# Deferring the merge of the two branches behind the sending of the softmax sums in a hybrid decoder layer

## The chip, the core and the metric

The kernel runs on one core of one Trainium2 chip. The metric is device time in microseconds (us) of one execution. TensorE is called PE, VectorE DVE, ScalarE ACT, GpSimd POOL and SyncE SP; SP computes nothing, it issues DMA transfers in its order. A line number (L1363) is one of the kernel before.

## What is computed

The layer is a half-step SwiGLU FFN, then two token mixers on one normalised input (a gated DeltaNet and a sparse attention), merged by sigmoid gates, then a second half-step FFN and a final RMSNorm; 1024 tokens, width 1024, 8 heads of 128. What the change touches is the end of the attention branch and the merge:

```
p = softmax(logits)            # per head and query, over the kept keys
o_sa = (p @ latent) @ w_uv     # per head
merged = sigmoid(gate_a) * o_dn + sigmoid(gate_b) * o_sa
x = x + merged @ w_o
```

## The kernel before, in words

Everything lies transposed in SBUF: channels on the 128 partitions, tokens along the free axis. The gated DeltaNet's output (`odd`), its gate product (`zgd`) and the attention gate (`gbd`) were written to DRAM in an earlier stage, as 8 heads x 128 x 1024.

The attention stage (`mixer`, its last block) runs `attn_head` for the 8 heads. One head handles 1024 queries in four units of 256 queries, in the order g = 0, 1, 3, 2; unit g has 2g+2 blocks of keys, so g = 3 is the longest and g = 0 the shortest. In a unit, for two blocks of 128 queries: PE makes the logits (`pl`), DVE adds bias and mask and takes the maximum (L1322), ACT makes the exponentials and their sums (`a_sum`, L1327). Then, for pairs of key blocks, PE transposes the probabilities (`pp`, L1335), ACT rounds them to the high part `ph` (L1338), DVE makes the rest `plo` (L1339), and PE multiplies by the values into `pao` (L139 to L141). ACT copies the unit's result to `osa` (L1344). The bias tile `nb` (L1309) is made by POOL. The probabilities are not divided by their sum; that is done in `merge`.

After units g = 1 and g = 2, when four of the eight query blocks have their sums, `merge` handles half a head, 512 queries. DVE makes `a_r` = 0.5 / sum as a 128 x 4 column tile (L1354, L1355), with queries on the partitions. The result `osa` has channels on the partitions, so the row of 512 values must stand on every partition: SP writes `a_r` to DRAM (`a_rd`, L1357; 512 packets of 4 bytes) and reads it back to all 128 partitions (`a_rb`, L1361, 256 KB). SP also loads `od`, `zg` and `gb` (256 KB each, L1361). POOL multiplies `od` by `zg` (L1362), DVE multiplies `osa` by `a_rb` (L1363) and by `gb` + 1 (L1364), POOL adds both into `merged` (tile `mr`, L1365). The landing tiles `od`, `zg`, `gb` and `a_rb` have one buffer each.

Around it: `attn_values` makes the values for two heads at once (weights `w_uv`, loaded to `w_raw` with two buffers, rounded by ACT at L111 and split by POOL at L112 to `wa`); `attn_qk` makes the next head's queries and keys (weights `w_uq`, `w_uk`), traced after unit g = 1 with a priority that moves it ahead. After the last head `merged` is split into high and low parts (`mh`, `ml`), and `out_proj` multiplies by `w_o` (`pwo`, L1377 adds it to `x`).

The order of instructions on each engine and on SP's queue is not the order of the source: the framework traces all of it and then places the instructions by priority (source order, if nothing else is said) and by the readiness that its own timeline forecasts. On the chip each engine, and SP, then runs its list in that order and waits where an operand is late. `issue_after(ins)` adds an edge for order alone: what is traced inside, on the engine of `ins`, is placed behind `ins`.

Of the kernel before, what the change touches and what calls it, by code (L numbers as in the profile page):

```python
# [10 lines left out]
F32 = mybir.dt.float32  # L11
# [4 lines left out]
ALU = mybir.AluOpType  # L16
# [4 lines left out]
P = 128  # L21
# [6 lines left out]
H = 8  # L28
# [42 lines left out]
class Layer:  # L71
# [1223 lines left out]
    def attn_head(self, hd, p, ps, qk, values, merged, ahead):  # L1295
        nc = self.nc
        near = self.near_tile(p, hd)
        (qh, ql), (kh, kl) = qk
        vh, vl = values
        hv = slice((hd % 2) * P, (hd % 2) * P + P)  # L1300
        sums = self.stat.tile([P, NT], F32, name="a_sum")
        osa = p.tile([P, S], F32, name="osa", tag="osa", bufs=2)
        for g in (0, 1, 3, 2):
            probs = []
            for b in (2 * g, 2 * g + 1):
                W = (b + 1) * P
                n_near = min(W, 256)
                nb = p.tile([P, 256], F32, name="nb", tag="nb", bufs=4)
                nc.gpsimd.tensor_add(nb[:, 256 - n_near:], near[:, 256 - n_near:], self.mask[b][:, W - n_near:W])  # L1309
                s = self.slot(("w_hi", "w_lo")[b % 2])  # L1310
                mx = self.stat.tile([P, 4], F32, name="a_mx", tag="a_mx", bufs=3)
                m = 0
                for n0 in range(0, W, 512):
                    n1 = min(W, n0 + 512)
                    pl = ps.tile([P, 512], F32, name="pl", tag="lg")
                    self.mm3(pl[:, 0:n1 - n0], qh[b // 4][:, ts(b % 4, P)], ql[b // 4][:, ts(b % 4, P)], kh[n0 // 512][:, 0:n1 - n0],
                             kl[n0 // 512][:, 0:n1 - n0], True, True)
                    for a0, a1 in ((n0, min(n1, W - n_near)), (max(n0, W - n_near), n1)):
                        if a1 <= a0:
                            continue  # L1320
                        add = nb[:, a0 - W + 256:a1 - W + 256] if a0 >= W - n_near else self.mask[b][:, a0:a1]
                        nc.vector.tensor_tensor_reduce(s[:, a0:a1], pl[:, a0 - n0:a1 - n0], add, 1.0,  # L1322
                                                       mx[:, m - 1:m] if m else -3.0e38, ALU.add, ALU.max, accum_out=mx[:, m:m + 1])
                        m += 1
                nm = self.stat.tile([P, 1], F32, name="a_nm", tag="a_nm", bufs=3)
                nc.vector.tensor_scalar_mul(nm, mx[:, m - 1:m], -1.0)
                nc.scalar.activation(s[:, 0:W], s[:, 0:W], AF.Exp, bias=nm, accum_out=sums[:, b:b + 1])  # L1327
                probs.append(s)
            po = ps.tile([P, 512], F32, name="pao", tag="ao")
            for j in range(0, 2 * g + 2, 2):  # L1330
                pt = ps.tile([P, 512], F32, name="pp", tag="pt")
                blocks = [(j, 0), (j, 1), (j + 1, 0), (j + 1, 1)] if j < 2 * g else [(j, 0), (j, 1), (j + 1, 1)]
                n = len(blocks) * P
                for i, (jj, b) in enumerate(blocks):
                    nc.tensor.transpose(pt[:, ts(i, P)], probs[b][:, ts(jj, P)], self.ident)  # L1335
                ph = p.tile([P, 512], F32R, name="ph", tag="ph", bufs=3)
                pl_ = p.tile([P, 512], F32R, name="plo", tag="plo", bufs=3)
                nc.scalar.copy(ph[:, 0:n], pt[:, 0:n])  # L1338
                nc.vector.tensor_sub(pl_[:, 0:n], pt[:, 0:n], ph[:, 0:n])  # L1339
                for i in range(2):  # L1340
                    a, b = (0, 256) if i == 0 else (256, n)
                    out = po[:, 0:256] if b - a == 256 else po[:, 128:256]
                    self.mm3(out, vh[:, j + i, hv], vl[:, j + i, hv], ph[:, a:b], pl_[:, a:b], j + i == 0, j + i == 2 * g + 1)
            nc.scalar.copy(osa[:, ts(g, 256)], po[:, 0:256])  # L1344
            if g == 1:
                ahead()
            if g in (1, 2):
                self.merge(hd, g // 2, sums, osa, p, ps, merged)

    def merge(self, hd, h, sums, osa, p, ps, merged):  # L1350

        nc = self.nc
        r = self.stat.tile([P, 4], F32, name="a_r")
        nc.vector.reciprocal(r, sums[:, ts(h, 4)])  # L1354
        nc.vector.tensor_scalar_mul(r, r, 0.5)  # L1355
        rd = self.dram.tile([512], F32, name="a_rd", tag="a_rd", bufs=2)
        nc.sync.dma_start(rd.rearrange("(t i) -> i t", i=P), r)  # L1357
        od, zg, gb, rb = (p.tile([P, 512], F32, name=n, tag=n, bufs=1) for n in ("od", "zg", "gb", "a_rb"))
        v = ts(h, 512)
        for x, src in ((od, self.odd[hd][:, v]), (zg, self.zgd[hd][:, v]), (gb, self.gbd[hd][:, v]), (rb, rd.partition_broadcast(P))):  # L1360
            nc.sync.dma_start(x, src)  # L1361
        nc.gpsimd.tensor_mul(od, od, zg)  # L1362
        nc.vector.tensor_mul(osa[:, v], osa[:, v], rb)  # L1363
        nc.vector.scalar_tensor_tensor(osa[:, v], gb, 1.0, osa[:, v], ALU.add, ALU.mult)  # L1364
        nc.gpsimd.tensor_add(merged[:, v], od, osa[:, v])  # L1365


    def out_proj(self, m, ps, after_tile, after_half):
# [53 lines left out]
    def run(self):  # L1422
        nc, tc, I = self.nc, self.tc, self.I
# [4 lines left out]
        self.zgd = dt([H, P, S], F32, name="zgd")  # L1428
        self.gbd = dt([H, P, S], F32, name="gbd")
        self.odd = dt([H, P, S], F32, name="odd")  # L1430
        self.parts, self.B = {}, {}
        hs = ExitStack()
        self.open_parts(hs, "hT", 0, NK, "right")
        with ExitStack() as c:
            ps = Banks(self.psum, s=(0, 1, 2, 3, 4, 5), m=(6, 7))
# [35 lines left out]
        merged, ms = self.mixer(hs)  # L1471
        with ExitStack() as c:
            ps = Banks(self.psum, s=(0, 1, 2, 3, 4, 5), m=(6, 7))
# [188 lines left out]
```

## Time and profile before

| | us |
|---|---|
| three executions | 2695.01, 2697.19, 2702.41 |
| median | 2697.19 |
| profiled execution, device time | 2702.38 |
| its span, first to last instruction | 2700.3 |
| around the span | 2.1 |
| attention stage, about 1616 to 1943 in the span | 327 |

Times in rows count from the start of the span. A row of a timeline has the start, the duration, the engine, the line, the operation with out<-in, and in brackets the idle time of that engine just before it and what ended it. A wait is put down to the releaser that came last. Two runs of before differ by up to 7.4 us.

### The profile page before, as it was taken

The numbers are of one execution on the slowest core, as the hardware profiler recorded it, in microseconds if no ns is written. First come the engines' busy times: TensorE is split into PE (matmuls) and PEld (weight loads), VectorE is DVE, ScalarE is ACT, GpSimd is POOL, SyncE is SP. The second block draws the span as 40 slices with busy tenths as digits, with TensorE's granted clock in tenths as the row PEclk, the third lists the DMA queues.
The fourth block names the chain that finished last, engine by engine and source line by source line (L and its number), as shares of the span: only waits on it lengthen the run. The fifth ranks groups of instructions, "written<-read, shape, count | busy, mean of one in ns | idle before, by whom it ended". The sixth has DMA issues, their size and how long they took to land.

```text
span 2700.3 us, 36120 instructions
## 1 busy us (share of the span) xinstructions
PE 2526.0 (94%) x12518; PEld 2061.8 (76%) x12518; DVE 1740.1 (64%) x3420; ACT 1200.0 (44%) x2338; POOL 972.7 (36%) x748
## 2 busy tenths in 40 slices
PE   6999999999989899989999999667798999999998
PEld 5788888888777688767787878567686888888886
DVE  7655555775655777999466846445558555556776
ACT  6444434323424665453477355334434344434333
POOL 5545543433533232232000013322346455543340
PEclk8999999999999899999999999888898999999999
DMA  5443337643343155355634223433452344347642
GB/s 165 134 145 137 118 128 266 243 160 124 97 119 104 51 140 141 90 137 127 207 125 131 88 86 71 68 68 65 138 163 82 110 145 137 101 164 261 218 159 76
DMA packets 376279, 356.94 MB, mean 132 GB/s; under 512 B 95961, under 2 KB 280097, under 8 KB 375073
## 3 DMA queue, kind: packets, MB, share of 16 engines
q1 hardware_dynamic: 372512, 348.87, 42.0%
q10 hardware_dynamic: 2304, 4.20, 0.4%
q0 software_dynamic: 1280, 1.57, 0.3%
q8 instruction: 99, 1.62, 0.3%
q14 instruction: 84, 0.68, 0.1%
HBM read 238.54 MB, written 116.01 MB: 131 GB/s over the span
## 4 chain that ended last, share of the span: by engine, by line
PE 36%; DVE 9%; DMA 9%; issue 2%; ACT 1%; POOL 1%; SPq 0%; DVEq 0%; POOLq 0%; ACTq 0%
PE pst L139 6%; PE pst L141 6%; PE pst L140 6%; DMA a_rd<-a_r 4%; PE pin L141 2%; PE pin L139 2%; PE pin L140 2%; DVE sb_p L1034 2%; PE pn L1221 1%; PE pv L1216 1%; PE po L1230 1%; DVE cv_y L923 1%; PE pwo L140 1%; PE pwo L141 1%; PE pwo L139 1%
## 5 line engine op out<-in xcount | busy, mean ns | idle before, releaser
L140 PE MATMUL pst<-p,w_hi 128*128 128x512 f32 x992 | 391.4, 395 | 8.3 <-DVE p L112 8.1
L139 PE MATMUL pst<-p,w_hi 128*128 128x512 f32 x992 | 393.0, 397 | 3.8 <-ACT p L111 1.9
L141 PE MATMUL pst<-p,w_hi 128*128 128x512 f32 x992 | 391.1, 395 | 0.4 <-DVE w_hi L112 0.2
L139 PE MATMUL pin<-p,w_hi 128*128 128x512 f32 (+1 forms) x848 | 342.4, 405 | 6.6 <-DVE cv_y L923 4.2
L111 ACT CAST w_hi<-w_raw 128x512 fp32r<-128x512 f32 (+3 forms) x294 | 204.1, 695 | 312.0 <-PE pst L141 135.4
L140 PE MATMUL pin<-p,w_hi 128*128 128x512 f32 (+1 forms) x848 | 340.9, 402 | 0.5 <-DVE p L112 0.5
L141 PE MATMUL pin<-p,w_lo 128*128 128x512 f32 (+1 forms) x848 | 341.1, 402 | 0.0
L112 DVE TENSOR_TENSOR w_lo<-w_raw,w_lo 128x512 fp32r<-128x512 f32 (+1 forms) x196 | 193.1, 987 | 169.4 <-ACT w_lo L111 167.6
L140 PE MATMUL pst<-p,w_lo 128*128 128x512 f32 x744 | 291.6, 392 | 3.7 <-DVE p L112 3.7
L141 PE MATMUL pst<-p,w_lo 128*128 128x512 f32 x744 | 291.5, 392 | 2.4 <-DVE w_lo L112 2.3
L139 PE MATMUL pst<-p,w_lo 128*128 128x512 f32 x744 | 289.8, 395 | 0.8 <-ACT c L360 0.5
L140 PEld LDWEIGHTS pst<-p,w_hi 128*128 128x128 f32 x992 | 187.9, 189 | 53.4 <-DVE p L112 12.4
L139 PEld LDWEIGHTS pst<-p,w_hi 128*128 128x128 f32 x992 | 188.4, 190 | 46.9 <-ACT p L111 3.4
L141 PEld LDWEIGHTS pst<-p,w_hi 128*128 128x128 f32 x992 | 188.2, 190 | 43.6 <-DVE w_hi L112 1.8
L111 ACT CAST w_lo<-w_raw 128x512 fp32r<-128x512 f32 (+1 forms) x200 | 115.8, 582 | 210.1 <-PE pst L141 92.1
L139 PEld LDWEIGHTS pin<-p,w_hi 128*128 128x128 f32 (+1 forms) x848 | 161.6, 191 | 43.8 <-DVE cv_y L923 4.5
L140 PEld LDWEIGHTS pin<-p,w_hi 128*128 128x128 f32 (+1 forms) x848 | 162.0, 191 | 37.6 <-issue 4.3
L141 PEld LDWEIGHTS pin<-p,w_lo 128*128 128x128 f32 (+1 forms) x848 | 161.3, 190 | 37.8 <-issue 3.9
L373 DVE TENSOR_TENSOR c<-c,pst 128x512 f32<-128x512 f32 x132 | 89.9, 683 | 148.2 <-PE pst L141 120.0
L112 POOL TENSOR_TENSOR w_lo<-w_raw,w_hi 128x1024 fp32r<-128x1024 f32 (+1 forms) x43 | 107.5, 2500 | 201.8 <-ACT w_hi L111 194.0
L141 PEld LDWEIGHTS pst<-p,w_lo 128*128 128x128 f32 x744 | 139.9, 188 | 35.5 <-DVE w_lo L112 4.2
L140 PEld LDWEIGHTS pst<-p,w_lo 128*128 128x128 f32 x744 | 139.9, 188 | 35.0 <-DVE p L112 4.9
(423 smaller groups left out, 5418.0 us busy)
## 6 DMA issues: line engine op xcount, KB each, us to landing
p<-mixd SPq DMA_DIRECT2D x144, 256.0 KB, 5.4
w_raw<-in_w_in_dram SPq DMA_DIRECT2D x52, 512.0 KB, 3.8
w_raw<-in_ffn_wg_dram SPq DMA_DIRECT2D x44, 512.0 KB, 3.6
w_raw<-in_ffn_wu_dram SPq DMA_DIRECT2D x44, 512.0 KB, 4.2
mixd<-t_hi SPq DMA_DIRECT2D x72, 256.0 KB, 4.4
mixd<-t SPq DMA_DIRECT2D x72, 256.0 KB, 3.6
w_raw<-in_ffn_wd_dram SPq DMA_DIRECT2D x48, 384.0 KB, 3.9
actd<-c SPq DMA_DIRECT2D x70, 256.0 KB, 3.3
```

The lines of the kernel that those rows point to most:

```text
L111: self.nc.scalar.copy(hi, raw)
L112: self.pin((self.nc.vector if engine == "vector" else self.nc.gpsimd).tensor_sub(lo, raw, hi))
L139: mm(ps, lhsT=wh, rhs=rh, start=first, stop=False, **kw)
L140: mm(ps, lhsT=wh, rhs=rl, start=False, stop=False, **kw)
L141: mm(ps, lhsT=wl, rhs=rh, start=False, stop=last, **kw)
L373: nc.vector.tensor_add(c[i, h], c[i, h], bank["y" if m == 1 else "z"])
L923: nc.vector.scalar_tensor_tensor(y[:, n:512], pps[h][:, 0:512 - n], cw[:, j:j + 1], y[:, n:512], ALU.mult, ALU.add)
L1034: nc.vector.tensor_mul(v, T[:, 0:i, 0:i].rearrange("p j c -> p c j"), L[:, None, 0:i, i].to_broadcast([P, i, i]))
L1216: nc.tensor.matmul(pv[r, i, :], lhsT=X[r, h, :], rhs=vb[r, h, :], start=True, stop=True)
L1221: nc.tensor.matmul(pn[:, i, :], lhsT=kd[r, h, :], rhs=vn[r, h, :], start=True, stop=True)
L1230: nc.tensor.matmul(po[r, i, :], lhsT=at[r, h, :], rhs=vn[r, h, :], start=True, stop=True)
```

## The change

`merge` now returns its last four instructions as a function `done`, and `attn_head` calls that function later: the one of g = 1 after unit g = 3 of the same head, the one of g = 2 after unit g = 1 of the next head. It is called inside `issue_after` with the unit's last `plo` subtraction, so its two DVE instructions stand behind that; its POOL instructions get no such edge. In `merge`, the loads of `od`, `zg` and `gb` are now traced ahead of the write `a_rd` instead of behind it. For the last half of the last head `done` follows at once, and the row of 512 values is not sent through DRAM: DVE scales the identity by each of the four columns of `a_r`, and PE multiplies a matrix of ones by it, which puts the row on all partitions of a PSUM bank.

```diff
-                nc.vector.tensor_sub(pl_[:, 0:n], pt[:, 0:n], ph[:, 0:n])
+                dve = nc.vector.tensor_sub(pl_[:, 0:n], pt[:, 0:n], ph[:, 0:n])
...
+            for late in self.outs:
+                late[0] -= 1
+            while self.outs and self.outs[0][0] == 0:
+                with self.tc.issue_after(dve.ins):
+                    self.outs.pop(0)[1]()
             if g in (1, 2):
-                self.merge(hd, g // 2, sums, osa, p, ps, merged)
+                out = self.merge(hd, g // 2, sums, osa, p, ps, merged)
+                if hd == H - 1 and g == 2:
+                    out()
+                else:
+                    self.outs.append([g, out])
...
-        rd = self.dram.tile([512], F32, name="a_rd", tag="a_rd", bufs=2)
-        nc.sync.dma_start(rd.rearrange("(t i) -> i t", i=P), r)
-        od, zg, gb, rb = (p.tile([P, 512], F32, name=n, tag=n, bufs=1) for n in ("od", "zg", "gb", "a_rb"))
+        od, zg, gb = (p.tile([P, 512], F32, name=n, tag=n, bufs=1) for n in ("od", "zg", "gb"))
         v = ts(h, 512)
-        for x, src in ((od, self.odd[hd][:, v]), (zg, self.zgd[hd][:, v]), (gb, self.gbd[hd][:, v]), (rb, rd.partition_broadcast(P))):
+        for x, src in ((od, self.odd[hd][:, v]), (zg, self.zgd[hd][:, v]), (gb, self.gbd[hd][:, v])):
             nc.sync.dma_start(x, src)
-        nc.gpsimd.tensor_mul(od, od, zg)
-        nc.vector.tensor_mul(osa[:, v], osa[:, v], rb)
-        nc.vector.scalar_tensor_tensor(osa[:, v], gb, 1.0, osa[:, v], ALU.add, ALU.mult)
-        nc.gpsimd.tensor_add(merged[:, v], od, osa[:, v])
+        if hd == H - 1 and h == 1:
+            rb = ps.tile([P, 512], F32, name="a_rp", tag="pt")
+            for t in range(4):
+                d = p.tile([P, P], F32, name="a_d", tag="near", bufs=2)
+                nc.vector.tensor_scalar_mul(d, self.ident, r[:, t:t + 1])
+                nc.tensor.matmul(rb[:, ts(t, P)], lhsT=self.ones, rhs=d, start=True, stop=True)
+        else:
+            rd = self.dram.tile([512], F32, name="a_rd", tag="a_rd", bufs=2)
+            nc.sync.dma_start(rd.rearrange("(t i) -> i t", i=P), r)
+            rb = p.tile([P, 512], F32, name="a_rb", tag="a_rb", bufs=1)
+            nc.sync.dma_start(rb, rd.partition_broadcast(P))
+
+        def done():
+            nc.gpsimd.tensor_mul(od, od, zg)
+            nc.vector.tensor_mul(osa[:, v], osa[:, v], rb)
+            nc.vector.scalar_tensor_tensor(osa[:, v], gb, 1.0, osa[:, v], ALU.add, ALU.mult)
+            nc.gpsimd.tensor_add(merged[:, v], od, osa[:, v])
+
+        return done
```

## Rows read from the trace of the kernel before

**Rows 1.** The page: chain that ended last, shares of the span by line.

```profile
PE pst L139 6%; PE pst L141 6%; PE pst L140 6%; DMA a_rd<-a_r 4%; PE pin L141 2%; PE pin L139 2%; PE pin L140 2%; DVE sb_p L1034 2%; PE pn L1221 1%; PE pv L1216 1%; PE po L1230 1%; DVE cv_y L923 1%; PE pwo L140 1%; PE pwo L141 1%; PE pwo L139 1%
```

**Rows 2.** Windows: the attention stage; length, busy time (instructions) by engine, clock, DMA.

```profile
core 0: us, PE busy (x) PEld busy (x) DVE busy (x) ACT busy (x) POOL busy (x), PEclk, DMA share, GB/s
1616.00:1943.00 327.00, 248.25 (x1476) 222.14 (x1476) 177.35 (x538) 145.13 (x322) 104.12 (x117) 0.85 0.35 72
```

**Rows 3.** Waits in the attention stage, engines: total us, times, longest.

```profile
POOL od L1362 <- DMA od<-odd: 79.9, 10, 12.6
...
DVE osa L1363 <- DMA a_rb<-a_rd: 65.2, 12, 9.3
...
ACT wa L111 <- DMA w_raw<-in_w_uv_dram: 25.1, 3, 13.3
```

**Rows 4.** Timeline of DVE, two heads, from one wait for weights to the next.

```profile
1726.41 0.69 DVE L1289 SCALAR_TENSOR_TENSOR p<-pqk,p 128x512 fp32r<-128x512 f32 x1 [11.18 <-ACT p L1288]
...
1755.57 0.69 DVE L1363 TENSOR_TENSOR osa<-osa,a_rb 128x512 f32<-128x512 f32 x1 [9.31 <-DMA a_rb<-a_rd]
...
1780.25 0.69 DVE L1363 TENSOR_TENSOR osa<-osa,a_rb 128x512 f32<-128x512 f32 x1 [7.31 <-DMA a_rb<-a_rd]
...
1792.17 0.69 DVE L1363 TENSOR_TENSOR osa<-osa,a_rb 128x512 f32<-128x512 f32 x1 [6.08 <-DMA a_rb<-a_rd]
...
1811.51 0.69 DVE L1289 SCALAR_TENSOR_TENSOR p<-pqk,p 128x512 fp32r<-128x512 f32 x1 [13.71 <-ACT p L1288]
```

**Rows 5.** Timeline of SP's queue in the same stretch.

```profile
1763.82 0.37 SPq L1357 DMA_DIRECT2D a_rd<-a_r  x1
...
1774.70 0.32 SPq L1361 DMA_DIRECT2D a_rb<-a_rd  x1
...
1775.55 0.42 SPq L1357 DMA_DIRECT2D a_rd<-a_r  x1
...
1797.30 0.38 SPq L1256 DMA_DIRECT2D w_raw<-in_w_uv_dram  x1
```

**Rows 6.** Timeline of ACT in the same stretch: ends of units, and the value weights.

```profile
1766.26 0.37 ACT L1344 COPY osa<-pao 128x256 f32<-128x256 f32 x1
...
1785.91 0.37 ACT L1344 COPY osa<-pao 128x256 f32<-128x256 f32 x1 [0.53 <-PE pao L141]
...
1810.36 0.62 ACT L111 CAST wa<-w_raw 128x512 fp32r<-128x512 f32 x1 [13.29 <-DMA w_raw<-in_w_uv_dram]
...
1812.15 0.38 ACT L1344 COPY osa<-pao 128x256 f32<-128x256 f32 x1
```

**Rows 7.** Waits in the attention stage, SP's queue: total us, times, longest.

```profile
SPq L1361 <- DMA a_rd<-a_r: 147.8, 16, 11.3
SPq L1361 <- POOL od L1362: 46.9, 12, 7.1
SPq L584 <- POOL nb L1309: 13.9, 3, 5.4
SPq L1361 <- POOL mr L1365: 12.7, 7, 5.7
SPq L1256 <- POOL wa L112: 10.3, 11, 2.5
SPq L1361 <- DVE a_mx L1322: 8.7, 3, 4.6
```

**Rows 8.** Timeline of SP's queue, ACT and PE at the end of the stage.

```profile
1930.73 0.32 SPq L1361 DMA_DIRECT2D a_rb<-a_rd  x1
...
1937.86 1.04 ACT L111 CAST w_hi<-w_raw 128x1024 fp32r<-128x1024 f32 x1 [7.49 <-DMA w_raw<-in_w_o_dram]
...
1939.34 0.58 PE L139 MATMUL pao<-ph,vh 128*128 128x256 f32 x1 [3.92 <-ACT ph L1338]
```

**Rows 9.** Groups by line, PE: a row of 128 values spread by a product.

```profile
L179 PE MATMUL n_rb<-ident,rs_y 128*128 128x128 f32 x80 | 11.9, 295 | 11.7 <-DVE rs_y L106 8.7 <-DVE sp_r L659 3.0
```

**Rows 10.** Timeline of DVE in the last head.

```profile
1907.82 0.69 DVE L1363 TENSOR_TENSOR osa<-osa,a_rb 128x512 f32<-128x512 f32 x1 [1.48 <-DMA a_rb<-a_rd]
...
1924.47 1.14 DVE L1339 TENSOR_TENSOR plo<-pp,ph 128x384 fp32r<-128x384 f32 x2
```

More of the change, by code (lines that the diff above doesn't have):

```diff
@@ L1430, in run @@
         self.odd = dt([H, P, S], F32, name="odd")
-        self.parts, self.B = {}, {}
+        self.parts, self.B, self.outs = {}, {}, []
         hs = ExitStack()
```

## The prediction

> **What bounds the kernel now.** I read the chain of waits first, then the busy times of the stage that it points to, then who waits there, and last the queues in order of time. Over the whole span the chain is TensorE's products, but one transfer of 2 KB stands among them: the write of the reciprocals to DRAM, 4% or some 108 us of 2700.3 [rows 1]. It occurs only in the attention stage, so that stage is to be read by itself. In its 327 us DVE is busy for 177.35, ACT for 145.13 and PE for 248.25 at a mean granted clock of 0.85, so part of the PE time is at 1.2 GHz instead of 2.4 [rows 2]. No engine is full: the stage is bound by waits. Of these, DVE stands 65.2 us in 12 waits for `a_rb`, POOL 79.9 us for `od`, ACT 25.1 us for the value weights `w_uv` [rows 3].
>
> Two heads repeat as one period, and the timeline shows what is in it: from 1726.41 to 1811.51, or 85.1 us, of which DVE waits 9.31 + 7.31 + 6.08 = 22.7 us for `a_rb` and 13.71 for what hangs on `w_uv` [rows 4]. DVE runs in order, so each wait for `a_rb` also holds the `plo` subtractions and maxima behind it, which PE needs. The reason is a round trip: a write at 1763.82 lets SP issue the read at 1774.70, and DVE goes on at 1780.25, 16.4 us after the write; the next write follows only at 1775.55 [rows 4, 5].
>
> **What the change does, part by part.**
>
> *The merge moved later.* The two DVE instructions and two POOL instructions of 15 merges move by one unit (g = 1) or two (g = 2). Their durations stay, so the gain is the wait alone. I replay the period with the three waits taken out. The first merge has its row by 1755.57; it is now due when unit g = 3 ends, 1766.26 - 9.31 = 1757: no wait [rows 4, 6]. The second is written at 1763.82 - 9.31 = 1754.5 and lands 16.4 later at 1770.9; it is due at the end of the next head's g = 1, 1785.91 - 9.31 - 7.31 = 1769.3: a wait of 1.6 [rows 4 to 6]. The third is due at 1812.15 - 22.7 + 1.6 = 1791.0. Its write went out 11.7 us after the second's, which gives a landing at about 1783; if SP puts its three loads first, which now wait for the second merge to end at some 1774, it lands at about 1774 + 16.4 = 1790.4: no wait either way [rows 4 to 6]. So 21.1 of 22.7 us could go.
>
> *What is late next: SP.* The writes stay. SP waits for a write's landing before it issues the read, and every load behind that waits too: 147.8 us in 16 waits [rows 7]. In a period that is 4 x (1774.70 - 1763.82) = 43.5 us [rows 5]. SP's other large waits are 46.9 + 13.9 + 12.7 + 10.3 + 8.7 = 92.5 us in 327, or 24.1 in 85.1 [rows 2, 7]. Sum 67.6: if none of them shrinks, SP lets a period fall by 17.5 us and no further. Ends for the gain of a period: 17.5 and 21.1. I take 17.5, since the loads of `od` wait for tiles that are now held for longer. Over the stage that is 65.2 x 17.5 / 22.7 = 50.3 us.
>
> A rule of the Trainium skill says otherwise of the round trip: "DMA: Bandwidth & Descriptors", section on the anatomy of one DMA, puts a transfer at about 2.0 us plus its bytes over 436 GB/s (fitted on GpSimd's path), which would be an estimate of 4.6 us for write and read. The trace shows 16.4, so the measurement decides; by the page SP could not bind, all 65.2 us would go, and the sum below would end near 2639.
>
> *Loads traced ahead of the write.* A write that is ready can now stand behind three loads that wait for their tiles. It is in the third merge above; beyond that zero, as the replay leaves that merge 8 us to spare in the one order and 0.6 in the other.
>
> *POOL.* `od` times `zg` and the last addition move with `done`, without an edge for order. If POOL's product is placed early, it waits for `od` as now, with `nb` and the weights' split behind it; I leave that cost as it is, and w_uv's 13.71 us per period too.
>
> *The last half head.* One write and one read go. The read, issued at 1930.73, held the loads of `w_o` back; ACT waited 7.49 us for one, with `ph` behind it, and PE 3.92 us for `ph` [rows 8]. I count the 3.92. Added: four scalings of 128 x 128, each at most the 0.69 of a 128x512 product, and four products at 0.295 [rows 4, 9]: at most 4.0 us in a chain. Between 0 (beside `out_proj`'s products) and 4.0 I take 2.6, as the chain stands ahead of `merged`.
>
> *The first half of the last head.* Its DVE product, at 1907.82, moves behind the last `plo` of unit g = 3, at 1924.47: 16.7 us later [rows 10]. `out_proj` needs it, but seven of its eight head blocks don't. Between 0 and 16.7 I take 8.4: no row tells which end is nearer. Naming the subtraction and the list of functions cost nothing on the chip.
>
> Sum: -50.3 - 3.9 + 2.6 + 8.4 = -43.2 us. The profiled execution took 2702.4 (2700.3 of span and 2.1 around it), so 2659.2; it lies 5.2 above the median of the three, so I predict **2654**. The clock is not counted: fewer PE pauses can only lift 0.85 towards 1, worth perhaps 0 to 8 us more.
>
> **Rivals.**
>
> *SP stays the bound.* The tiles `od`, `zg`, `gb` and `a_rb` have one buffer, and each is now held for a unit longer. If SP's waits for POOL [rows 7] grow by two thirds of what DVE's shrink, some 20 us of the 65.2 go, less the 7.1 that the last head costs by the sum above: 13 us, **2684**. For it: 147.8 us of SP's waits, of which 15/16 stay. Against it: the replay, in which every row lands by its due time. The same page, in the same section, says that a semaphore wait is done by the issuing sequencer before the transfer is dispatched; SP's 147.8 us agree, and by that rule a deferred reader frees nothing on SP.
>
> *Slower: weights behind a held tile.* The place is SP's list around 1797, where `w_uv` goes out directly behind a merge's transfers [rows 5]. If the weights' loads of a head are placed behind a load of `od` that waits for a `done`, they wait for about a unit. The third merge's tiles, worked on from 1792.17 now, would be so from 1812.15, which is 20.0 us later, or 6.3 without the 13.71 for `w_uv` [rows 4, 6]; with 13, the middle, two heads lose 26 us per period against 21.1 saved, and 4.9 x 65.2 / 22.7 is +14: **2711**. It decides from the point where weights come 10.6 us later per head than now; ACT already waits 13.29 for them [rows 6], so nothing covers it.
>
> *The change doesn't do what it says.* The forecast that orders the lists takes other times for a transfer than the chip; if it moves other DVE work ahead of `done` by as much, or puts `done` directly behind a short unit while the row is late by SP's queue, the waits stay: **2697**.
>
> **How the numbers follow.** Forecast 0.58, SP the bound 0.20, unchanged 0.09, slower 0.13. A measurement of this kernel tells 0.3% (8 us) from no change; forecast and first rival lie below 2689, so faster is 0.78, same 0.09, slower 0.13. The low end takes the replay's 21.1 per period (-10.3), no loss at the first half (-8.4) and the clock (-8): 2627. The high end takes in the first rival with its own spread, to 2692; what lies beyond is 0.13 of slower, part of unchanged, and a little below.
>
> **What would show it.** Right: DVE's waits for `a_rb` fall from 65.2 to under 20 us, the stage from 327 to some 285, its clock rises above 0.85, SP's wait for the landing stays near 140, the product of the last half no longer follows a read. Wrong: SP's waits for POOL's `od` or `mr` grow by tens of us, or ACT's for `w_uv` above 40; or `out_proj` stands idle for over 10 us for the last head's first half.

## The result, and the profile after

The changed kernel takes 2653.77 us (median of four, 2650.71 to 2657.82); the kernel before, in four executions beside it, 2696.1 (2694.02 to 2702.41). The ratio is 0.984 with a 95% interval of 0.9819 to 0.9861: 1.6% faster, some 42 us. The forecast of 2654 is met in its total. Its two main terms are not: both are wrong, and their errors cancel.

| profiled execution | before, us | after, us | difference |
|---|---|---|---|
| device time | 2702.38 | 2654.08 | -48.3 |
| start of the span to the first `w_uv` load that SP issues in the stage | 1636.11 | 1631.18 | -4.9 |
| to the second `w_uv` load (two heads) | 76.64 | 72.76 | -3.9 |
| to the third (two heads) | 84.55 | 69.14 | -15.4 |
| to `a_r` of the first half of the last head | 94.11 | 81.37 | -12.7 |
| to the last product `osa` | 51.19 | 40.70 | -10.5 |

The first difference lies ahead of all that the change touches; what comes behind the last product `osa` keeps its length to within 1 us. The marks come from the timelines of SP and DVE. Those that aren't shown in the rows ahead are, of the kernel before:

```profile
1636.11 0.38 SPq L1256 DMA_DIRECT2D w_raw<-in_w_uv_dram  x1
...
1712.75 0.43 SPq L1256 DMA_DIRECT2D w_raw<-in_w_uv_dram  x1
...
1891.41 0.17 DVE L1354 RECIPROCAL a_r<-a_sum 128x4 f32<-128x4 f32 x1
...
1942.60 0.69 DVE L1363 TENSOR_TENSOR osa<-osa,a_rb 128x512 f32<-128x512 f32 x1 [0.84 <-ACT osa L1344]
```

The period of the working answers to this stretch of DVE's timeline after the change ([rows 4] before); the last three rows are of the last head: the reciprocals and the product of its first half, which [rows 10] has before, and the product of its second:

```profile
1714.30 0.69 DVE L1289 SCALAR_TENSOR_TENSOR p<-pqk,p 128x512 fp32r<-128x512 f32 x1 [12.58 <-ACT p L1288]
...
1743.16 0.69 DVE L1384 TENSOR_TENSOR osa<-osa,a_rb 128x512 f32<-128x512 f32 x1 [0.40 <-DMA a_rb<-a_rd]
...
1756.36 0.69 DVE L1384 TENSOR_TENSOR osa<-osa,a_rb 128x512 f32<-128x512 f32 x1 [1.76 <-DMA a_rb<-a_rd]
...
1769.61 0.69 DVE L1384 TENSOR_TENSOR osa<-osa,a_rb 128x512 f32<-128x512 f32 x1 [4.27 <-DMA a_rb<-a_rd]
...
1784.16 0.69 DVE L1289 SCALAR_TENSOR_TENSOR p<-pqk,p 128x512 fp32r<-128x512 f32 x1 [12.53 <-ACT p L1288]
...
1854.45 0.17 DVE L1364 RECIPROCAL a_r<-a_sum 128x4 f32<-128x4 f32 x1
...
1880.00 1.31 DVE L1384 TENSOR_TENSOR osa<-osa,a_rb 128x512 f32<-128x512 f32 x1
...
1895.15 0.69 DVE L1384 TENSOR_TENSOR osa<-osa,a_rp 128x512 f32<-128x512 f32 x1
```

From 1714.30 to 1784.16 it is 69.9 us long instead of 85.1. The waits for the row fall from 22.7 to 6.4 us, where the replay left 1.6; the wait for the weights stays (12.53 for 13.71). The queue of SP ([rows 5] before), with its loads of the value weights as marks, tells why the waits don't vanish:

```profile
1631.18 0.38 SPq L1256 DMA_DIRECT2D w_raw<-in_w_uv_dram  x1
...
1703.94 0.38 SPq L1256 DMA_DIRECT2D w_raw<-in_w_uv_dram  x1
...
1727.77 0.42 SPq L1378 DMA_DIRECT2D a_rd<-a_r  x1
1739.50 0.33 SPq L1380 DMA_DIRECT2D a_rb<-a_rd  x1
1740.90 0.37 SPq L1378 DMA_DIRECT2D a_rd<-a_r  x1
1752.15 0.32 SPq L1380 DMA_DIRECT2D a_rb<-a_rd  x1
1753.47 0.42 SPq L1378 DMA_DIRECT2D a_rd<-a_r  x1
1764.51 0.32 SPq L1380 DMA_DIRECT2D a_rb<-a_rd  x1
1765.83 0.42 SPq L1378 DMA_DIRECT2D a_rd<-a_r  x1
1773.08 0.38 SPq L1256 DMA_DIRECT2D w_raw<-in_w_uv_dram  x1
1778.49 0.32 SPq L1380 DMA_DIRECT2D a_rb<-a_rd  x1
```

Each write follows the read of the merge before it by 1.3 to 1.4 us: four round trips stand back to back and fill 50.7 of the 69.9 us, 11 to 13 each. Before, the trips had gaps: the write at 1763.82 [rows 5] came 11.5 us after the read of the merge before it (1752.30). After the change SP has no such gap among the four. The first of them goes out within 0.1 us of its `a_r` on DVE, and the next three 3.2, 5.8 and 4.4 us after theirs: they queue on SP. One gap is left behind the fourth read (19.9 us, to the next write at 1798.41), and the write that ends it waits for its `a_r`.

The waits of the stage after the change, engines and then SP's queue (total us, times, longest):

```profile
POOL od L1383 <- DMA od<-odd: 62.3, 9, 14.7
...
ACT wa L111 <- DMA w_raw<-in_w_uv_dram: 36.5, 3, 17.7
...
DVE osa L1384 <- DMA a_rb<-a_rd: 26.7, 9, 6.3
```

```profile
SPq L1369 <- POOL od L1383: 91.0, 15, 12.5
SPq L1380 <- DMA a_rd<-a_r: 85.2, 12, 11.2
```

DVE's 65.2 us [rows 3] are now 26.7. SP's wait for the landing fell from 147.8 to 85.2 [rows 7], though as many writes are made but one: part of it turned into the wait for POOL's `od`, 46.9 before and 91.0 now. Together these two are 194.7 us of the 327 before and 176.2 of the 288 looked at now, 60% and 61%. SP stands in these two waits for the same share of a shorter stage. The windows of the old stage and of the period above, with the columns of [rows 2]:

```profile
1616.00:1943.00 327.00, 281.85 (x1688) 246.74 (x1688) 202.91 (x560) 154.75 (x333) 113.58 (x120) 0.92 0.40 107
1704.00:1773.00 69.00, 56.45 (x360) 50.10 (x360) 42.37 (x132) 32.61 (x77) 24.68 (x29) 0.89 0.35 77
```

The first now holds work of `out_proj` as well. In the period the granted clock is 0.89, where it was 0.85 in that of the kernel before (1713 to 1797). In the chain of waits the write to DRAM has come down from 4% [rows 1] to 2%.

### The profile page after: what moved, and what is told of

It is laid out like the page before. It is cut to its first block, busy times and chain, and to the rows that moved or that the text cites. A ratio compares the mean times of both kernels' runs of the same rounds, so it can differ in the third digit from the quotient of the medians.

```text
span 2652.1 us, 36132 instructions
## 1 busy us (share of the span) xinstructions
PE 2519.1 (95%) x12526; PEld 2054.9 (77%) x12526; DVE 1737.9 (66%) x3424; ACT 1198.3 (45%) x2338; POOL 970.9 (37%) x748
## 4 chain that ended last, share of the span: by engine, by line
PE 40%; DVE 9%; DMA 6%; issue 2%; ACT 1%; POOL 1%; SPq 0%; DVEq 0%; POOLq 0%; ACTq 0%
PE pst L139 7%; PE pst L141 7%; PE pst L140 7%; PE pin L141 2%; PE pin L139 2%; PE pin L140 2%; DVE sb_p L1034 2%; DMA a_rd<-a_r 2%; DMA od<-odd 1%; PE pn L1221 1%; PE po L1230 1%; PE pv L1216 1%; DVE cv_y L923 1%; PE pq L1211 1%; PE pwo L141 1%
## 5 line engine op out<-in xcount | busy, mean ns | idle before, releaser
L140 PEld LDWEIGHTS pst<-p,w_hi 128*128 128x128 f32 x992 | 188.3, 190 | 53.9 <-DVE p L112 12.9
```

The costliest lines, as they stand in the source:

```text
L140: mm(ps, lhsT=wh, rhs=rl, start=False, stop=False, **kw)
```

## The experiments

They ran on other chips than the profiles above; there the kernel before takes 2670 to 2675 us. So each kernel is compared by its ratio to the kernel before beside it. The period is the time between the second and third load of `w_uv` in SP's timeline, one pair of heads. The kernel before has 84.55 on the first chip; on these, e1 and e4 stand for it, whose heads are those of the kernel before.

| kernel | us | ratio, 95% interval | period |
|---|---|---|---|
| e1, last half head alone | 2667.87 | 0.9978, 0.9964 to 0.9992 | 78.9 |
| e2, deferral alone | 2636.13 | 0.9861, 0.9838 to 0.9885 | 63.2 |
| e3, TensorE for all, at once | 2614.78 | 0.9788, 0.9761 to 0.9814 | 57.9 |
| e4, no edge | 2668.54 | 0.9985, 0.9967 to 1.0002 | 79.7 |
| e5, e3 with an unused trip | 2667.94 | 0.9969, 0.9957 to 0.9981 | 76.3 |
| e6, second `zg` | 2634.10 | 0.9851, 0.9830 to 0.9871 | 65.2 |
| e7, one unit later still | 2635.82 | 0.9854, 0.9834 to 0.9874 | 67.2 |
| e9, e3 with second `od`, `zg` | 2621.78 | 0.9801, 0.9781 to 0.9821 | 58.0 |
| e10, TensorE for all, deferred | 2619.06 | 0.9796, 0.9769 to 0.9823 | 57.1 |
| e11, e3 with an unused write | 2631.88 | 0.9847, 0.9824 to 0.9869 | 67.3 |
| e12, e10 with an unused trip | 2643.63 | 0.9888, 0.9864 to 0.9912 | 68.8 |
| e13, the change again | 2633.24 | 0.9852, 0.9829 to 0.9874 | 65.1 |

e1 to e4 shared a chip, e5, e6, e7 and e9 another, e10 to e13 a third.

### Which part of the change does it

**e1** is the kernel before with nothing but the new last half head:

```diff
+        end = hd == H - 1 and h == 1
+        if not end:
+            rd = self.dram.tile([512], F32, name="a_rd", tag="a_rd", bufs=2)
+            nc.sync.dma_start(rd.rearrange("(t i) -> i t", i=P), r)
...
+        if end:
+            rb = ps.tile([P, 512], F32, name="a_rp", tag="pt")
...
```

> The kernel before, with one part of the change: the last half of the last head spreads its sums with the identity and TensorE, and nothing is deferred. My theory: the gain comes from DVE no longer standing for 15 round trips, so this part alone gives the 3.9 us that PE waited behind the held loads of w_o, less up to 2.6 us of new work: 2692 to 2697. Rival (the end of the stage is where the time went, since the changed kernel's last head went from its sums to its last product in 40.7 us instead of 51.2): 2684 to 2688.

**e2** is the changed kernel with the last half head sent through DRAM like the others:

```diff
-        if hd == H - 1 and h == 1:
+        if False:
```

> The changed kernel, but the last half of the last head sends its sums through DRAM like the other 15; the merge is deferred as in the change. My theory: nearly all of the gain stays, 2654 to 2660, and DVE's waits for the returned row stay near 27 us. Rival (the end of the stage): 2664 or more.

**e4** is the changed kernel without the edge for order:

```diff
-                with self.tc.issue_after(dve.ins):
-                    self.outs.pop(0)[1]()
+                self.outs.pop(0)[1]()
```

> The changed kernel without the edge that places the two late DVE instructions behind the unit's last subtraction; they are only traced later. If the edge does the work, the list puts them back to where the row is forecast to have landed, DVE's waits return to 50 to 65 us and the time to 2680 to 2697. If tracing later is enough (my guess, since source order is the priority): 2650 to 2662, waits for the row within 10 us of the changed kernel's 26.7.

The expectations of e1 to e4 are put in the times of the first chip; with its 2696 us the ratios of e1, e2 and e4 are 2690, 2659 and 2692. e2 has the whole gain: 0.9861, against 0.9852 for the change itself (e13). DVE's waits for the row are 10.6 us in e2, not near 27; they are 10.6 in e13 too, so that is the chip and not the edit. e1 alone gives 0.2% (0.08 to 0.36), about 6 us, which is less than such a run can tell inside the change; it lies between its two expectations and settles neither. And e4 is e1: the order of instructions on every engine and on SP's queue is the same in both kernels, and so is the time. Tracing `done` a unit or two later moves nothing, because the framework places its instructions where its forecast says that they are ready; the edge alone pushes them back. Counted in the lists of the first 15 merges, 518 DVE instructions in all stand between the reciprocals `a_r` and their product `osa` in the kernel before, in e1 and in e4, and 725 in the changed kernel. My guess for e4 was wrong, and the other case that I had named came.

### Is it DVE's wait for the row, or SP's trip

**e3** makes the row of every merge on TensorE, with a helper of the kernel that spreads a column by four products, and asks for no deferral. Nothing goes through DRAM:

```diff
-        rd = self.dram.tile([512], F32, name="a_rd", tag="a_rd", bufs=2)
-        nc.sync.dma_start(rd.rearrange("(t i) -> i t", i=P), r)
...
+        rb = self.spread(r, p, ps, "pt")
```

> The kernel before with no round trip at all: each of the 16 merges puts its row on all partitions with four TensorE products, at once, and the merge is not deferred; no write to DRAM and no read back. My theory (the round trip holds DVE, and SP behind it): the 65.2 us of DVE's waits and SP's 147.8 us go, so the time falls below the changed kernel's, to some 2615 to 2640. Rival (the stage is held by the single-buffered tiles and by POOL's wait for od): DVE's waits move to gb or od and the time stays above 2655.

By its ratio e3 is at 2639 on the first chip, in the range of its theory. Its lists are not those of the kernel before without the trip, though: the framework places the products of the first 15 merges later on DVE, 658 instructions behind their `a_r`, where it is 518 before and 725 in the change. So e3, and e5 and e11 with it, are in part deferred by the list itself.

**e5** is e3 with the write and the read still made, into a tile that nothing uses. DVE never waits for the row; SP has all its transfers and its wait for the landing:

```diff
         rb = self.spread(r, p, ps, "pt")
+        rd = self.dram.tile([512], F32, name="a_rd", tag="a_rd", bufs=2)
+        nc.sync.dma_start(rd.rearrange("(t i) -> i t", i=P), r)
+        un = p.tile([P, 512], F32, name="a_rb", tag="a_rb", bufs=1)
-        for x, src in ((od, self.odd[hd][:, v]), (zg, self.zgd[hd][:, v]), (gb, self.gbd[hd][:, v])):
+        for x, src in ((od, self.odd[hd][:, v]), (zg, self.zgd[hd][:, v]), (gb, self.gbd[hd][:, v]), (un, rd.partition_broadcast(P))):
```

> As the kernel in which every merge spreads its row with TensorE at once (2615 us on this series' chip), but the write to DRAM and the read back are still made, 16 times, and nobody uses what they bring. DVE waits for no row; SP still stands for each landing, with the loads of od, zg, gb and the weights behind it. My theory (after the change SP's chain of writes and reads is the next bound): the time comes back most of the way to the deferred kernel, 2630 to 2655 there. Rival (only DVE's wait mattered): within 8 us of the kernel without the trip, 2607 to 2623.

**e11** is e5 without the read, so SP waits for no landing:

```diff
-        un = p.tile([P, 512], F32, name="a_rb", tag="a_rb", bufs=1)
-        for x, src in ((od, self.odd[hd][:, v]), (zg, self.zgd[hd][:, v]), (gb, self.gbd[hd][:, v]), (un, rd.partition_broadcast(P))):
+        for x, src in ((od, self.odd[hd][:, v]), (zg, self.zgd[hd][:, v]), (gb, self.gbd[hd][:, v])):
```

> Every merge spreads its row with TensorE at once; the 512 values are also written to DRAM in packets of 4 bytes, but not read back, so SP never stands for a landing while the packets still go through the same queue. With the read back it was 2668, without both 2615. If SP's standing makes the price (my theory): 2612 to 2625. If the packets themselves hold up the transfers behind them on the queue: 2640 or more.

The three differ on SP's queue alone; the lists of PE, DVE, ACT and POOL are the same. Of e3's gain of 2.1%, the trip that nobody uses takes back 1.8% (0.9788 to 0.9969, some 48 us), and the write alone 0.6% (to 0.9847, some 16 us, give or take 9). e5 came out slower than the 2655 at which its theory ended, and e11 between its two ranges: the write alone has a price, and the larger part comes with the read, that is with SP's standing and the read's own 256 KB, which no run parts. And e5, in which DVE has no wait for the row at all, is within its interval as fast as e1 (0.9969 and 0.9978), in which DVE waits for it still: the waits of e1 say

```profile
DVE osa L1374 <- DMA a_rb<-a_rd: 48.1, 10, 7.2
```

So some 48 us of DVE's waits are taken away in e5 and next to nothing is gained (e5 has 60 products more on PE, and its lists are those of e3). Where they went, the waits of e5 in the stage show:

```profile
POOL od L1364 <- DMA od<-odd: 58.5, 6, 12.9
...
DVE plo L1339 <- ACT ph L1338: 45.3, 17, 12.3
...
ACT wa L111 <- DMA w_raw<-in_w_uv_dram: 22.8, 3, 11.6
...
DVE w_hi L1322 <- POOL nb L1309: 17.5, 3, 6.3
```

and in the timelines of ACT and DVE one of them in place:

```profile
1711.95 0.62 ACT L111 CAST wa<-w_raw 128x512 fp32r<-128x512 f32 x1 [11.58 <-DMA w_raw<-in_w_uv_dram]
...
1713.09 1.29 DVE L1339 TENSOR_TENSOR plo<-pp,ph 128x512 fp32r<-128x512 f32 x2 [12.28 <-ACT ph L1338]
```

ACT waits 11.58 us for a load of weights that SP issues late, and DVE 12.28 us for `ph`, which stands behind that on ACT. POOL waits for `od`, and DVE for `nb`, which stands behind that on POOL. In e1 the four lines are 71.2, 16.9, 21.4 and 1.7 us: the waits of POOL for `od` and of ACT for the weights are not longer in e5, but DVE's for `ph` and `nb` have grown by 44.2 us, nearly the 48.1 that went. In e3 the same waits are small:

```profile
DVE plo L1339 <- ACT ph L1338: 12.8, 16, 4.3
...
POOL od L1361 <- DMA od<-odd: 16.7, 7, 3.9
```

The trips on SP's queue pace the stage of e5, and they reach the engines by several ways. `a_rb` on DVE was the place where they showed, not their only way in: the other operands of a merge, and the weights, stand behind the same landing. SP's waits and queue in e5:

```profile
SPq L1363 <- DMA a_rd<-a_r: 130.4, 16, 9.9
```

```profile
1724.83 1.72 SPq L1360 DMA_DIRECT2D a_rd<-a_r  x1
1736.51 0.34 SPq L1363 DMA_DIRECT2D a_rb<-a_rd  x1
...
1737.61 0.42 SPq L1363 DMA_DIRECT2D od<-odd  x1
```

`od` goes out 12.8 us after the write, behind a read that nobody uses, and `gb` (1736.90) just ahead of it.

The unread write costs through what goes out beside it on the queue. From issue to landing of `od` in the stage (queue, transfers, KB each, median us) with no write, the write alone, and the whole trip, that is e3, e11 and e5:

```profile
od<-odd SPq DMA_DIRECT2D x15, 256.0 KB, 2.8
```

```profile
od<-odd SPq DMA_DIRECT2D x15, 256.0 KB, 3.8
```

```profile
od<-odd SPq DMA_DIRECT2D x15, 256.0 KB, 5.1
```

The median hides the worst of it. In e11, where SP waits for no write to land, an `od` that goes out between two writes (the second at 1743.47) keeps POOL waiting to 1757.28, and POOL's waits for `od` are nearly four times those of e3:

```profile
1743.04 0.32 SPq L1362 DMA_DIRECT2D od<-odd  x1
```

```profile
1757.28 1.26 POOL L1363 TENSOR_TENSOR od<-od,zg 128x512 f32<-128x512 f32 x1 [14.26 <-DMA od<-odd]
```

```profile
POOL od L1363 <- DMA od<-odd: 63.6, 8, 14.3
```

In e3 the longest of these waits is 3.9 us. SP also stands 13.5 us for `a_r` ahead of the writes of e11, which e3 does not; how much of the 16 us that makes was not tried.

### What the trip costs once the merge is deferred

**e10** is the changed kernel with the row from TensorE, copied by DVE into the tile `a_rb`, and no trip:

```diff
-            rd = self.dram.tile([512], F32, name="a_rd", tag="a_rd", bufs=2)
-            nc.sync.dma_start(rd.rearrange("(t i) -> i t", i=P), r)
             rb = p.tile([P, 512], F32, name="a_rb", tag="a_rb", bufs=1)
-            nc.sync.dma_start(rb, rd.partition_broadcast(P))
+            nc.vector.tensor_copy(rb, self.spread(r, p, ps, "pt"))
```

> The changed kernel with no round trip: the deferred merges take their row from four TensorE products and a DVE copy to the landing tile, made at once, instead of from DRAM. Deferral and edge stay. The last result was that the trip made by SP alone, used by nobody, gave back nearly all that spreading by TensorE had gained (0.997 of before against 0.979), where merges are not deferred. If deferral takes the uses off SP's late loads, what is left of the trip's price is 10 to 20 us: 2615 to 2626 where the changed kernel has 2636. If deferral hides the trip entirely, 2630 to 2640 (15 copies of 0.69 us are added).

**e12** is e10 with the write and the read still made, unused:

```diff
+            rd = self.dram.tile([512], F32, name="a_rd", tag="a_rd", bufs=2)
+            nc.sync.dma_start(rd.rearrange("(t i) -> i t", i=P), r)
+            un = p.tile([P, 512], F32, name="un", tag="n_un", bufs=1)
+            nc.sync.dma_start(un, rd.partition_broadcast(P))
```

> As the deferred kernel that takes its row from TensorE, but write and read back are still made by SP and nobody uses them. The engines' lists are the same as in that kernel. Against the changed kernel it shows what DVE's remaining wait for the row costs (10 to 27 us of waits in three profiles), against the deferred kernel without the trip what SP's standing still costs. My theory: SP's standing makes most of it, 2628 to 2640; rival (the row's lateness makes it): 2612 to 2625.

**e13** is the changed kernel, unaltered, on the same chip.

> The changed kernel unaltered, on the chip of these runs, to compare with: by its ratio of 0.984 to the kernel before, 2632 to 2640 if the kernel before stands at 2675 again.

e10 comes out as expected. With the deferral the trip costs 0.9% (0.9796 to 0.9888, 24.6 us), half of the 1.8% without the edge; e12 is 3.6 us above the range of its theory. And in neither e5 nor e12 does anyone wait for a row through DRAM, yet deferring the merge is worth 0.8% there too (0.9969 to 0.9888). So the edge buys more than the row's arrival. A likely reason is that all operands of `done` that the landing delays, `gb` and `od` among them, get a unit's grace, and DVE and POOL, which run in order, don't hold up the next unit; as e5 and e12 also differ in where SP's list has the loads around the write, this is argued and not shown. The waits of e12 against those of e5 agree in part: DVE's for `ph` fall from 45.3 to

```profile
DVE plo L1339 <- ACT ph L1338: 17.8, 17, 4.1
```

and those for POOL's `nb`, 17.5 us in e5, are gone; against that, DVE's for ACT's `p` rise from 18.6 to 33.0. Which of the operands matters most was not taken apart.

e13 uses the row that e12 throws away and is 10.4 us faster (2633.24 and 2643.63; e12 has 15 copies and 60 products more). So whatever the row's own lateness still costs in the changed kernel, it is 10.4 us less than those copies and products; DVE's waits for it are 10.6 us in e13. With e10's row and no trip the kernel takes 14.2 us less than e13 (2619.06), in spite of the copies and products.

### Is there more in the deferral

**e7** defers each merge by one unit more, except in the last head, and **e6** gives `zg` a second buffer, so that its load need not wait for the held product:

```diff
-                    self.outs.append([g, out])
+                    self.outs.append([g + (hd < H - 1), out])
```

> The changed kernel with every deferred merge one unit later still (two and three units; the last head as in the change). DVE's waits for the row, 26.7 us in the changed kernel, can then go to under 5; against that, od, zg, gb and the row's tile are held for a unit longer, and SP's loads of the next merge wait for them. If DVE's wait is still the bound: 10 to 20 us faster than the changed kernel. If SP's chain is the bound (my theory): no faster than the changed kernel, 0 to 25 us slower, and SP's waits for POOL and DVE grow.

```diff
-        od, zg, gb = (p.tile([P, 512], F32, name=n, tag=n, bufs=1) for n in ("od", "zg", "gb"))
+        od, zg, gb = (p.tile([P, 512], F32, name=n, tag=n, bufs=1 + (n == "zg")) for n in ("od", "zg", "gb"))
```

> The changed kernel with two buffers for zg instead of one, nothing else. After the change SP waits 91.0 us for POOL to have used od and zg, where it waited 46.9 before. If that held the stage, two buffers free SP by some 5 us per merge and the time falls by 10 to 25 us against the changed kernel. If SP only waits there instead of for the landing that comes next (85.2 us after the change, 147.8 before), the time stays within 5 us; I hold this for likelier, since the write's landing and not the load of zg is what the row needs.

**e9** is e3 with two buffers for `od` and `zg`:

```diff
-        od, zg, gb = (p.tile([P, 512], F32, name=n, tag=n, bufs=1) for n in ("od", "zg", "gb"))
+        od, zg, gb = (p.tile([P, 512], F32, name=n, tag=n, bufs=1 + (n != "gb")) for n in ("od", "zg", "gb"))
```

> The kernel in which every merge spreads its row with TensorE at once, with two buffers for od and zg (the space of the row's landing tile, which it no longer needs, pays for one). It showed SP waiting 75.7 us for DVE and 51.4 us for POOL to free the tiles. If those waits delay the weights behind them, 3 to 10 us faster than the one with single buffers; if they are idle time of a queue that is not the bound (my guess, as its PE runs at 0.98 of the clock in the stage), within 3 us.

e7 and e6 stand where the change stands (0.9854, 0.9851, 0.9852), e9 no better than e3 (0.9801 and 0.9788). In e7 the time came out as its theory had it, and little else did: DVE's waits for the row stay (10.8 us, 10.6 in e13), SP's for POOL's `od` fall (49.2, from 80.5). And SP hardly stands for a landing any more, since the list has other transfers between a write and its read. Its wait in e13 and in e7:

```profile
SPq L1380 <- DMA a_rd<-a_r: 68.6, 12, 8.7
```

```profile
SPq L1380 <- DMA a_rd<-a_r: 8.1, 1, 8.1
```

So 60 us of SP's standing are gone in e7 and no time is gained. The writes and reads are still made, and e11 has shown that writes alone slow what goes out beside them. In the changed kernel, then, the trip's remaining price is likelier in its transfers than in SP's standing; as all the lists of e7 differ from those of e13, this is not shown. Sending the trip through another engine's queue, which might part the two, was not tried.

SP's waits for tiles that POOL still holds grew with the change, but waits of that kind need not bind: in e3 SP stands 127.1 us for tiles,

```profile
SPq L1360 <- DVE osa L1363: 75.7, 13, 11.1
SPq L1360 <- POOL od L1361: 51.4, 15, 4.7
```

and cost nothing there, since a queue that has been served early stands too. e6 moves only one load in SP's list, so it is a weak test of the buffers by itself; a second `od` and `gb` in the changed kernel was not tried.

The fastest version is **e3**, simpler than the change and 0.6% ahead of it by the ratios (0.9788 and 0.9852, on different chips): some 17 us; e9 and e10 lie within its interval. Its period in the windows of the trace, with the same period of e13 below it:

```profile
1687.00:1745.00 58.00, 56.32 (x394) 51.76 (x393) 41.95 (x134) 33.67 (x77) 24.48 (x29) 1.00 0.24 71
```

```profile
1692.00:1757.00 65.00, 57.10 (x360) 51.40 (x360) 42.58 (x132) 32.76 (x77) 25.76 (x30) 0.88 0.35 82
```

PE is busy for 56.32 of 58 us, at the full clock: with the trips gone the period is bound by TensorE, though it has 34 matmul instructions more (the spread's products count as two each). At 0.88 of the clock e13's PE takes longer for fewer of them (57.10 us for 360), so a part of the trips' price is likely paid through the clock.

## Why the prediction was right, and where it was wrong

**What bounds the stage** was read rightly: waits, with the round trip of the reciprocals behind them, and the deferral with its edge frees DVE from most of it. The rival "doesn't do what it says" was a near thing, as e4 shows: without the edge it would have come true, for the reason that it named, that the list follows the forecast and not the source.

**The period** was put at 85.1 - 17.5 = 67.6 us, by SP's sum and not by the 21.1 of DVE's replay; it measured 69.9. Preferring the queue that issues to the engine that waits was the step that held: the four trips took 46.7 us from write to read, put at 43.5, and the rest 23.2, put at 24.1. The parts agree less well than that, since SP's waits for POOL's `od`, counted in the rest, now lie in part within the trips. The replay by itself failed: it timed the writes by the units of work, but once DVE is free the trips queue on SP, and the third row of the period is 4.27 us late where the replay had it in time.

**From the period to the stage** is the step that failed: "65.2 x 17.5 / 22.7 is 50.3" takes the gain to be proportional to DVE's waits for `a_rb`. The heads gave 3.9 + 15.4 + 12.7 = 32.0 us. In the first two heads 18.3 us of such waits stood before and 12.1 still stand, and 3.9 us were gained; the period that I had replayed was the one with the most to give. In the three stretches of the table the waits for the row fell by 6.2, 16.3 and 12.9 us, not far from what was gained: what failed is the share that goes, 34%, 72% and 61% instead of one share of 77% for all. That waits and gain go together here is no rule either: in e5 these waits are taken away entirely without a gain.

**The end of the stage** was put at -3.9 + 2.6 + 8.4 = +7.1 and measured -10.5. The loads of `w_o` come earlier: ACT's longest wait for one is 4.3 us after, 7.49 before. The new chain on DVE and PE is short; the groups by line have it at

```profile
L1374 DVE TENSOR_SCALAR a_d<-ident,a_r 128x128 f32<-128x128 f32 x4 | 1.0, 278 | 0.0
...
L1375 PE MATMUL a_rp<-a_d,ones 128*128 128x128 f32 x8 | 1.2, 274 | 0.0
```

with no idle time ahead of either, 2.2 us against the bound of 4.0; DVE goes straight from another instruction, which ends at 1895.14, to the product that needs the row. The later half did no harm: its product came 25.5 us after `a_r` (1854.45 to 1880.00) instead of 16.4, so 9.1 us later where 16.7 was feared, and PE then stands only 1.2 us in two waits for DVE's part of the split of `merged`, where before it stood 8.88 us for POOL's part, as PE's timeline of the kernel before has it:

```profile
1913.17 0.79 PE L140 MATMUL pwo<-ml,w_hi 128*128 128x512 f32 x1 [8.88 <-POOL ml L112]
```

I had not read this wait of the kernel before, which is the largest of PE there. PE's clock rises in this stretch as well, from 0.83 to 0.92. How much of the 10.5 is the TensorE row stays open: alone it is worth 0.2% (e1), and inside the change e2 and e13 don't tell it from nothing.

**The two errors**, 18 us too much in the heads and 18 too little at the end, cancel; that the total came out to a microsecond is luck and no proof of the working. The profiled runs differ by 4.9 us more ahead of the stage; the 5.2 that I took off to get to the median happens to make up for that.

**The rivals.** "SP stays the bound" was right that the trips on SP's queue go on costing time, and wrong in how much. Its sign came (SP's wait for POOL's `od` rose by 44 us), and e10 against e12 shows the trips on SP's queue still costing 24.6 us, though e7 speaks against SP's standing as the reason; but that wait came in place of the wait for the landing, not on top of it. The forecast that the latter would stay near 140 fell: it is 85.2. DVE's waits for the row are 26.7, not under the 20 that I had set as a sign. "Weights behind a held tile" did not come: ACT's waits for `w_uv` went from 25.1 to 36.5 us, below the 40 that I had set, and the third `w_uv` load now stands ahead of a row's read in SP's queue. The clock rose as said, from 0.85 in the period before to 0.89; no row had priced the 0 to 8 us that I gave it, and no run parts it from the rest.

**The length of a trip.** The trace has a landing of 11.5 us for the 2 KB write after the change. The Trainium skill, "DMA: Bandwidth & Descriptors", section on the anatomy of one DMA, would by its fit (for GpSimd's path) make the whole trip an estimate of 4.6 us and SP free; the trips of 11 to 13 us on SP's queue above decide against that. The Trainium skill's other rule there is that the issuing sequencer does a semaphore wait before the transfer is dispatched; that agrees with SP's waits for the landing of a write ahead of the read, 85.2 us after the change. That a deferred reader then frees nothing on SP was my inference, and it held for the change, where SP's share of waiting is 60% before and 61% after, but not for e7, whose list puts the read later.

## What to carry to other kernels

A wait on a compute engine tells where lateness shows, not what removing it is worth: before counting it as gain, ask what the queue behind the late operand would do to the next consumer, and, where it can be made, run the kernel with the operand made another way and the transfers kept. Here deferring the reader won back 1.5% of the 2.1% that a slow round trip cost, and making the row of 512 with four small products on TensorE removed it. In a framework that orders by forecast, code moved in the source alone may move nothing; compare the order of the instructions before expecting anything of the time, also where an edit seems to leave the order alone, as in e3.

## What the runs showed of the hardware

A write of 2 KB that nobody reads or waits for is not free: as 512 packets of 4 bytes, 16 of them cost some 16 us of time (e11 against e3, give or take 9). Loads of `od` beside them land at a median of 3.8 instead of 2.8 us, and one of them only some 14 us after its issue. That this is due to the packets and not to the bytes was not tried. Its own landing varies more than the kernels do: a median of 10.3 us in e1 and of 9.5 in e4, which have the same lists and ran on one chip, so the 10.9 us of [rows 5] should not be read to the tenth. And with the trips gone, TensorE's granted clock is 1.00 (2.4 GHz) in the whole period of e3, with PE busy for 97% of it; in the period of e13, with PE busy for 88%, it is 0.88, a mixture of the two levels. The busy share alone does not tell the clock: in the period of e11 (1692 to 1759) PE is busy for 89% and the clock is 0.99.
